# A mixture-of-experts decoder on one core: seven of eight experts sorted by token count, four of them in plain float32, gathers one expert ahead

## The chip, the cores and the metric

The kernel runs on one core of one Trainium2 chip. The time is device microseconds of one execution, and lower is better. The profile is of one execution of its own.

## What is computed

Two decoder layers on 256 tokens of 1024 features: an RWKV-7 time mix with a dense SwiGLU, then an RG-LRU block with a top-2-of-8 expert SwiGLU, and a last norm. All weights and activations are float32. The change lies in the expert layer alone:

```python
def moe_swiglu(h, w_router, b_router, w_gu, w_d):      # h: 256 tokens x 1024
    t = h.reshape(B * T, D)
    logits = t @ w_router + b_router                     # 8 experts
    top_v, top_i = lax.top_k(logits, 2)
    comb = einsum('nk,nke->ne', softmax(top_v), one_hot(top_i, 8))
    for e in range(8):                                   # w_gu[e]: 1024 x 7168, w_d[e]: 3584 x 1024
        out = out + comb[:, e, None] * swiglu(t, w_gu[e], w_d[e])
```

256 tokens with two experts each make 512 rows, 64 for each expert in the mean. With the inputs as drawn by the reference the counts of experts 0 to 7 are 59, 75, 55, 76, 73, 57, 51 and 66.

## The kernel before

The expert layer is the last stage. It runs 8 positions `e` one after the other, each of `NJ` = 7 steps `j` over 512 of the 3584 hidden columns: 56 steps `s` in all. A step takes 6 tiles of 1 MB of weights: two for gate, two for up, two for down (the down tiles of step `s` come behind the gate and up tiles of step `s+1`). `Stream` (line 100) loads them through SP's queue into a ring of 12 buffers; a load is issued when the tile 12 places before it is free.

Positions come in two kinds.

- A *large* position holds up to 128 tokens. Each tile is cut in two pieces of 1024 columns. ScalarE rounds a piece to float32r (`wh`), VectorE makes the rest (`wl`), and TensorE adds three float32r products (`mm3`). The step has 72 products of 512 columns and four transposes of the hidden tile (`hp`). A raw tile is free when VectorE has split its second piece. `Stream.next` emits the splits four pieces ahead, with five pairs of buffers.
- A *small* position (those in `SMALL` = 2, 5, 7) holds up to 64 tokens. Its tiles go to TensorE as they are, as plain float32 products of 512 columns whose two halves of the output columns fill the two halves of the array. A raw tile is free when TensorE has read it. There is nothing to split.

Experts 0 and 1 run at positions 0 and 1. Experts 2 to 7 are ranked by their token counts on VectorE (`t_rank`, `t_sel`), and `TURN` gives the rank of each position 2 to 7, so that the three with the fewest tokens come to positions 2, 5 and 7. The order of kinds is L L S L L S L S. From position 2 on the address of a weight load comes from a register of SP, which `turns()` (emitted behind step 4) loads from `turn_i`. A count over 64 in a small position or over 128 in a large one sets `cmx`, and the kernel then runs `overflow` (line 269) at its end, for each expert that has too many tokens, with all its weights loaded again.

Tokens are gathered by a product with a 0/1 matrix `Pm`. Two neighbouring positions are gathered together: 32 products of 256 columns in float32r (`gather_mm`: 8 feature tiles, high and low part, two token tiles), then ScalarE scales and shifts (`gather_mod`), rounds (`gather_out`), and VectorE makes the low part. For positions 0 and 1 this is `first_gather`, in front of the stage; for the others `gather(pair)` is emitted at the last step of an odd position. `scatter_cols` transposes `Pm` for the way back. At the end of a position, `expert_out` weighs the down result, splits it and adds it onto the tokens (`onto`: `sc` tiles, two products for each of four parts).

Small work (`expert_out`, `choice`, `scatter_cols`, the ranking) stands in the list `chores`; `chore()` takes one from it in front of each piece of a large position, and as often in a small one. Everything that isn't held to program order is ordered by the tile scheduler; each engine then runs its own queue in order. The PSUM tiles of `hp`, `gp` (gather), `sc` and `ptp` take banks 4 and 5 by turns.

Of the kernel before, what the change touches and what calls it, by code (L numbers as in the profile page):

```python
# [16 lines left out]
P = 128  # L17
# [11 lines left out]
SMALL = (2, 5, 7)  # L29
HALF = 64  # L30

TURN = (3, 0, 1, 4, 2, 5)
# [310 lines left out]
def kernel_body(tc, io, out, dbg=None):  # L343
# [18 lines left out]
    with ctx:  # L362
# [1042 lines left out]
        turn_i = rw.tile([P, E - 2], I32, name="turn_i")  # L1405
# [5 lines left out]
        crank, turnf = wrs[:, 2, 0:E - 2], wrs[:, 3, 0:E - 2]  # L1411
        oscr = cst2[:, 0:72].rearrange("p (i a b) -> p i a b", i=2, a=E - 2)
        sel = cst2[:, 72:108].rearrange("p (a b) -> p a b", a=E - 2)
# [247 lines left out]
        def as_numbered(w, e, *j):  # L1661
            return w[(e, *j)]

        add_steps(0, 2 * NJ, as_numbered)
# [15 lines left out]
        def onehot(Pm, i, pair, behind=None):  # L1680

            for z in range(2):
                e = 2 * pair + z
                pm, at, ps_, ms_ = Pm[:, i, z, :], iota, *((posq, mskq) if pair else (posm, msk))
                if e in SMALL:

                    pm, at = pm.rearrange("p (a c) -> p a c", a=2), iota[:, None, 0:HALF].broadcast_to([P, 2, HALF])
                ins = V.tensor_scalar(pm, at, ps_[:, i, e:e + 1], ms_[:, i, e:e + 1], ALU.is_equal, ALU.mult)
                if behind is not None:
                    order(tc, ins, behind)  # L1690
            return ins
# [38 lines left out]
        gps = [pg.tile([P, 2, 2 * CAP], F32, tag="g", name=f"gp0{k2}") for k2 in range(4)]  # L1730
        Pm = rp.tile([P, 2, 2, CAP], F32R, name="Pm0")
# [72 lines left out]
        def first_gather(i, ks, parts=range(2)):  # L1804
            for k in ks:
                for z in parts:
                    gather_mm(gps[k // 2][:, k % 2, :], (hh, hl)[z], i, k, Pm, i == 0 and k % 2 == 0 and z == 0,
                              i == 1 and k % 2 == 1 and z == 1)
# [80 lines left out]
        ma = ml.enter_context(tc.tile_pool(name="moe2", bufs=1))  # L1889

        spare = cst3
        xg, xfs = {}, {}
# [4 lines left out]
        def gather_mod(pair, k2, ps, eng=(0, 1)):  # L1897

            a = ma.tile([P, 2, 2 * CAP], F32R, tag=f"xh{k2}", name=f"xh{pair}{k2}")
            b = ma.tile([P, 2, 2 * CAP], F32R, tag=f"xl{k2}", name=f"xl{pair}{k2}")  # L1900
            xg.setdefault(pair, []).append((a, b))

            if pair == 0:
                xf = rr[:, 2 * k2:2 * k2 + 2, :]
            else:
                xf = (ma.tile([P, 512], F32, tag="xf", name=f"xf{pair}{k2}") if k2 % 2 == 0 else spare).rearrange("p (k c) -> p k c", k=2)
            xfs[k2] = xf
            for kk in range(2):
                k = 2 * k2 + kk
                if eng[kk]:  # L1910
                    V.tensor_scalar(xf[:, kk, :], ps[:, kk, :], mod(1, 4, k), mod(1, 3, k), ALU.mult, ALU.add)
                else:
                    S.activation(xf[:, kk, :], ps[:, kk, :], AF.Identity, bias=mod(1, 3, k), scale=mod(1, 4, k))

        def gather_out(pair, k2):

            a, b = xg[pair][k2]
            zs = [z for z in range(2) if 2 * pair + z not in SMALL]
            cs = slice(zs[0] * CAP, (zs[-1] + 1) * CAP)
            S.copy(a[:, :, cs], xfs[k2][:, :, cs])  # L1920
            V.tensor_tensor(b[:, :, cs], xfs[k2][:, :, cs], a[:, :, cs].bitcast(F32), ALU.subtract)
            for z in range(2):
                if z not in zs:
                    S.copy(xsm[2 * pair + z][:, 2 * k2:2 * k2 + 2, :], xfs[k2][:, :, z * CAP:z * CAP + HALF])

        for k2 in range(4):
            if k2 == 0:
                gather_mod(0, 0, gps[0])
            if k2 < 3:
                gather_mod(0, k2 + 1, gps[k2 + 1])  # L1930
            gather_out(0, k2)
            if k2 == 2:
                more(1)
                later()
# [8 lines left out]
        def scatter_cols(pair, z, eng):  # L1943
            ps = pdn.tile([P, 2, P], F32, tag="m", name=f"ptp{pair}{z}", bufs=2)
            for i in range(2):
                TE.transpose(ps[:, i, :], Pms[pair][:, i, z, :].bitcast(F32), ident)
            PT = ma.tile([P, 2, P], F32R, tag="PT", name=f"PT{pair}{z}", bufs=2)
            eng(PT, ps)
            PTs[2 * pair + z] = PT

        def choice(pair, i):
            if i == 0:
                Pms[pair] = mb.tile([P, 2, 2, CAP], F32R, tag="Pm", name=f"Pm{pair}")
            onehot(Pms[pair], i, pair, st.split[1])


        N6 = E - 2
        o6 = oscr.rearrange("p a b c -> p (a b c)")[:, 0:N6 * N6].rearrange("p (b c) -> p b c", b=N6)

        def t_rank():  # L1960

            a_, b_ = cnt[:, None, 2:E].broadcast_to([P, N6, N6]), cnt[:, 2:E, None].broadcast_to([P, N6, N6])
            V.tensor_tensor(o6, a_, b_, ALU.is_equal)
            V.tensor_tensor(o6, o6, lt8[:, 2:E, 2:E], ALU.mult)
            V.tensor_tensor(sel, a_, b_, ALU.is_gt)
            V.tensor_tensor(o6, o6, sel, ALU.add)
            V.tensor_reduce(crank, o6, AX.X, ALU.add)

        def t_sel():
            for k, r in enumerate(TURN):  # L1970
                V.tensor_scalar(sel[:, k, :], crank, float(r), None, ALU.is_equal)
            V.tensor_tensor(o6, sel, iota[:, None, 2:E].broadcast_to([P, N6, N6]), ALU.mult)
            V.tensor_reduce(turnf, o6, AX.X, ALU.add)
            V.tensor_copy(turn_i, turnf)

        def t_sort(dst, src):
            V.tensor_copy(dst[:, :, 0:2], src[:, :, 0:2])
            V.tensor_tensor(oscr, src[:, :, None, 2:E].broadcast_to([P, 2, N6, N6]),
                            sel[:, None, :, :].broadcast_to([P, 2, N6, N6]), ALU.mult)
            V.tensor_reduce(dst[:, :, 2:E], oscr, AX.X, ALU.add)  # L1980

        def t_cap():

            V.memset(cap, float(CAP))
            V.tensor_scalar(cap[:, 2:E], crank, float(N6 - len(SMALL)), None, ALU.is_ge)
            V.tensor_scalar(cap[:, 2:E], cap[:, 2:E], float(HALF - CAP), float(CAP), ALU.mult, ALU.add)
# [7 lines left out]
        def turns():  # L1994
# [3 lines left out]
            def by_turn(w, e, *j):  # L1998
                if e < 2:
                    return as_numbered(w, e, *j)  # L2000
                return w[(bass.ds(regs[e - 2], 1), *j)].rearrange("o p n -> (o p) n")

            add_steps(2 * NJ, len(steps), by_turn)
# [3 lines left out]
        def gather(pair):  # L2007

            for k2 in range(KT // 2):
                ps = pdn.tile([P, 2, 2 * CAP], F32, tag="m", name=f"gp{pair}{k2}", bufs=2)  # L2010
                for kk in range(2):
                    for z, src in enumerate((hh, hl)):
                        for i in range(2):
                            gather_mm(ps[:, kk, :], src, i, 2 * k2 + kk, Pms[pair], z == 0 and i == 0, z == 1 and i == 1)
                gather_mod(pair, k2, ps, (0, 0))
                gather_out(pair, k2)

        def gu_half(e, ps):
            xs = xg[e // 2]
            for q in range(4):  # L2020
                chore()
                wh, wl = st.next()
                for kk in range(2):
                    k = 2 * q + kk
                    cs = slice((e % 2) * CAP, (e % 2) * CAP + CAP)
                    mm3(ps, xs[q][0][:, kk, cs], xs[q][1][:, kk, cs],
                        wh[:, kk * 512:(kk + 1) * 512], wl[:, kk * 512:(kk + 1) * 512], k == 0, k == KT - 1)

        def gu_small(e, ps):

            for h in range(2):
                w = [st.next() for _ in range(2)]
                for k4 in range(4):
                    chore()
                    k = 4 * h + k4
                    for z in range(2):
                        mm(ps[z * HALF:(z + 1) * HALF], xsm[e][:, k, :], w[z][:, k4 * 512:(k4 + 1) * 512], k == 0, k == KT - 1)
# [44 lines left out]
        def expert_out(e):  # L2082
# [5 lines left out]
            def weigh(n):  # L2088
                yg[n] = ma.tile([P, 512], F32, tag="xf", name=f"yg{e}{n}") if n == 0 else spare
# [9 lines left out]
            def onto(n, i):  # L2099
# [7 lines left out]
                V.scalar_tensor_tensor(xt[:, i, sl], ps, (cmbq if e > 1 else cmb)[:, i, e:e + 1], xt[:, i, sl], ALU.mult, ALU.add)  # L2107
# [14 lines left out]
        def expert_out_small(e):  # L2122

            yg = ma.tile([P, 512], F32, tag="xf", name=f"yg{e}")
# [74 lines left out]
        for s, (e, j) in enumerate(steps):  # L2199
# [5 lines left out]
            if s == 0:  # L2205
                for z in range(2):
                    scatter_cols(0, z, S.copy)
# [197 lines left out]
```

## Time and profile before

| | us |
|---|---|
| median of 3 runs | 1537.98 (1536.16 to 1539.76) |
| the profiled execution | 1536.94 |
| its span, first to last instruction | 1534.8 |
| of it, up to the first gate product of the expert layer | 617.15 |
| expert layer up to its last down product | 902.6 |
| rest of the span | 15.0 |

The rows that the prediction uses stand in numbered groups in a later section. In rows of groups of instructions, the columns are the line (96 is the helper that records each operation), engine, operation, output <- inputs by the program's names, shapes, count, then busy us and mean ns of one, then idle us of the engine before them and what ended it. Products of one accumulation are pipelined, so the mean of one is longer than the distance from one to the next; that is read from the chain of waits, where a line gives start, duration and count of a run of products.

### The profile page before, as it was taken

To read this page: it belongs to the slowest core of one execution; us is meant where nothing else is said; L and a number is where in the kernel's file an instruction comes from. 1 tells how busy PE (TensorE), PEld (TensorE's weight loads), DVE (VectorE), ACT (ScalarE), POOL (GpSimd) and SP (SyncE) were. 2 spreads that over 40 slices of the span, in tenths; PEclk is the share of its full clock that TensorE was granted. 3 is DMA by queue.
4 is the path that set the end of the run, shared out by engine and by line. 5 is a ranking of instruction groups with operands and counts; after the bars stand their busy time and mean duration, and the time that the engine had idled before them with its cause. 6 is when DMAs were issued, how large, how long until landed. Compare 5 with 4: busy or idle time off the path is not lost.

```text
span 1534.8 us, 21180 instructions
## 1 busy us (share of the span) xinstructions
PE 1455.3 (95%) x7887; PEld 1070.1 (70%) x7887; DVE 1102.6 (72%) x1612; ACT 834.5 (54%) x1202; POOL 52.7 (3%) x44
## 2 busy tenths in 40 slices
PE   4998898999999898999999999999999999999996
PEld 3774684999999897878888534688788533688432
DVE  7788977788886887999999412887898512788302
ACT  3657434444444675877777412676777303577101
POOL 3011700000000000000000000000000000000000
PEclk9999989999999999999999999999999999999999
DMA  9563336988988345799999799999899899999796
GB/s 377 182 233 137 111 111 269 364 301 325 339 303 321 138 158 198 268 364 370 366 354 359 316 416 421 421 421 386 313 363 375 332 391 421 420 421 386 302 420 256
DMA packets 69936, 488.55 MB, mean 318 GB/s; under 512 B 8000, under 2 KB 8384, under 8 KB 11968
## 3 DMA queue, kind: packets, MB, share of 16 engines
q1 hardware_dynamic: 69824, 487.11, 82.2%
q8 instruction: 64, 1.05, 0.3%
q14 instruction: 48, 0.39, 0.1%
HBM read 486.03 MB, written 1.05 MB: 317 GB/s over the span
## 4 chain that ended last, share of the span: by engine, by line
PE 81%; DVE 8%; DMA 5%; ACT 4%; issue 1%; SPq 0%; POOL 0%; DVEq 0%; ACTq 0%
PE mg L96 20%; PE dn L96 16%; PE mu L96 13%; PE fgu L96 11%; PE fd L96 5%; DMA rw<-moe_gu 4%; PE psr L96 2%; PE linx L96 2%; DVE rq L96 2%; PE u L96 1%; PE hp L96 1%; DVE wl L96 1%; PE psk L96 1%; PE sc L96 1%; DMA rq<-ada 1%
## 5 line engine op out<-in xcount | busy, mean ns | idle before, releaser
L96 DVE TENSOR_TENSOR wl<-rw,wh 128x1024 fp32r<-128x1024 f32 x528 | 626.6, 1221 | 81.9 <-ACT wh L96 75.5
L96 ACT CAST wh<-rw 128x1024 fp32r<-128x1024 f32 x528 | 542.5, 1051 | 188.6 <-PE fgu L96 44.6
L96 PE MATMUL mg<-rw,condr 128*64 128x512 f32 x672 | 160.6, 595 | 2.2 <-DMA rw<-moe_gu 2.2
L96 DVE TENSOR_TENSOR sl<-sl,mg 64x512 f32<-64x512 f32 x21 | 14.5, 692 | 163.4 <-ACT sl L96 163.4
L96 PE MATMUL fgu<-fxh,wh 128*128 128x256 f32 x448 | 127.2, 285 | 1.2 <-ACT fxh L96 1.2
L96 PE MATMUL fgu<-fxl,wh 128*128 128x256 f32 x448 | 127.2, 284 | 0.0
L96 PE MATMUL fgu<-fxh,wl 128*128 128x256 f32 x448 | 126.6, 283 | 0.0
L96 PE MATMUL mg<-wl,xh 128*128 128x512 f32 x280 | 113.8, 406 | 7.9 <-DVE wl L96 7.8
L96 PEld LDWEIGHTS mg<-rw,condr 128*64 128x64 f32 x672 | 49.5, 137 | 98.2 <-issue 92.0
L96 PE MATMUL mg<-wh,xh 128*128 128x512 f32 x280 | 111.0, 396 | 2.9 <-ACT wh L96 2.9
L96 PE MATMUL dn<-wl,hTh 128*128 128x512 f32 x280 | 111.3, 398 | 0.6 <-DVE wl L96 0.6
L96 PE MATMUL dn<-wh,hTl 128*128 128x512 f32 x280 | 111.6, 399 | 0.0
L96 PE MATMUL mu<-wh,xh 128*128 128x512 f32 x280 | 111.3, 397 | 0.0
L96 PE MATMUL mg<-wh,xl 128*128 128x512 f32 x280 | 110.5, 394 | 0.2 <-DVE xl L96 0.2
L96 PE MATMUL mu<-wl,xh 128*128 128x512 f32 x280 | 110.2, 394 | 0.0
L96 PE MATMUL mu<-wh,xl 128*128 128x512 f32 x280 | 109.7, 392 | 0.0
L96 PE MATMUL dn<-wh,hTh 128*128 128x512 f32 x280 | 99.8, 398 | 0.7 <-ACT hTh L96 0.7
L96 ACT ACTIVATE sl<-mg 128x512 f32<-128x512 f32 (+1 forms) x56 | 32.9, 588 | 123.8 <-PE mg L96 123.7
L96 PEld LDWEIGHTS fgu<-fxh,wh 128*128 128x128 f32 x448 | 84.8, 190 | 2.0 <-ACT fxh L96 1.6
L96 PE MATMUL dn<-rw,hTh 128*64 128x512 f32 x336 | 84.9, 599 | 0.5 <-ACT hTh L96 0.5
L96 PEld LDWEIGHTS fgu<-fxl,wh 128*128 128x128 f32 x448 | 84.9, 190 | 0.7 <-issue 0.5
L96 PEld LDWEIGHTS fgu<-fxh,wl 128*128 128x128 f32 x448 | 85.2, 190 | 0.2 <-issue 0.2
(416 smaller groups left out, 2464.9 us busy)
## 6 DMA issues: line engine op xcount, KB each, us to landing
rw<-moe_gu SPq DMA_DIRECT2D x224, 1024.0 KB, 7.5
rw<-moe_d SPq DMA_DIRECT2D x106, 1024.0 KB, 7.9
rw<-ffn_gu SPq DMA_DIRECT2D x28, 1024.0 KB, 7.4
rw<-ada SPq DMA_DIRECT2D x28, 1024.0 KB, 7.8
rq<-ada SPq DMA_DIRECT2D x19, 1024.0 KB, 5.1
rw<-ffn_d SPq DMA_DIRECT2D x14, 1024.0 KB, 6.3
rw<-lru_in SPq DMA_DIRECT2D x8, 1024.0 KB, 7.4
rw<-moe_d SPq DMA_DIRECT2D x12, 512.0 KB, 15.0
```

Of the source, the lines that this page charges most:

```text
L96: r = f(*a, **k)
```

## The change

- Position 0 holds expert 7 (`FIRST`). The experts 0 to 6 are ranked, and positions 1, 3, 5 and 7 hold the four with the fewest tokens as small ones: L S L S L S L S. The ranking works on 7 x 7 instead of 6 x 6. `turns()` stands behind step 3 instead of 4.
- Tokens are gathered for one position at a time: 32 products of 128 columns for a large position, of 64 for a small one. `first_gather` serves position 0 alone. The gather for position `e+1` goes through `chores` while position `e` runs: from its step 2 in a large one, from step 1 in a small one, in two blocks of 16 products, with ScalarE's part as further chores. A large position's gather goes into two PSUM tiles of four feature tiles each, a small one's into one.
- `scatter_cols` is called for each position.
- The tiles of gathered tokens are half as wide, and small positions share one. The room goes to one more ring buffer (`rawD`): 13.

```diff
-SMALL = (2, 5, 7)
+FIRST = E - 1
+SMALL = (1, 3, 5, 7)
-TURN = (3, 0, 1, 4, 2, 5)
+TURN = (3, 0, 4, 1, 5, 2, 6)
...
-        add_steps(0, 2 * NJ, as_numbered)
+        add_steps(0, NJ, of_first)
...
         def gather_mm(o, src, i, k, Pm, start, stop):
-            mm(o, src[:, i, k * P:(k + 1) * P], Pm[:, i, :, :].rearrange("p z c -> p (z c)"), start, stop)
+            mm(o, src[:, i, k * P:(k + 1) * P], Pm[:, i, 0:o.shape[-1]], start, stop)
...
-        gps = [pg.tile([P, 2, 2 * CAP], F32, tag="g", name=f"gp0{k2}") for k2 in range(4)]
-        Pm = rp.tile([P, 2, 2, CAP], F32R, name="Pm0")
+        gps = [pg.tile([P, 4, CAP], F32, tag="g", name=f"gp0{k4}") for k4 in range(2)]
+        Pm = rp.tile([P, 2, CAP], F32R, name="Pm0")
...
-        first_gather(1, range(2), range(1))
-        first_gather(1, range(2), range(1, 2))
-        first_gather(1, range(2, 8))
+        first_gather(1, range(4), range(1))
+        first_gather(1, range(4), range(1, 2))
+        first_gather(1, range(4, 8))
...
+        st.grow(ml.enter_context(tc.tile_pool(name="rawD", bufs=1)))
-        spare = cst3
+        spare, other = cst3, condr[:, KT * HALF:D]
-        xsm = {e: condr[:, n * 512:(n + 1) * 512].rearrange("p (k c) -> p k c", k=KT) for n, e in zip((0, 1, 0), SMALL)}
+        xsm = condr[:, 0:KT * HALF].rearrange("p (k c) -> p k c", k=KT)
...
-        def gather(pair):
-            for k2 in range(KT // 2):
-                ps = pdn.tile([P, 2, 2 * CAP], F32, tag="m", name=f"gp{pair}{k2}", bufs=2)
-                for kk in range(2):
-                    for z, src in enumerate((hh, hl)):
-                        for i in range(2):
-                            gather_mm(ps[:, kk, :], src, i, 2 * k2 + kk, Pms[pair], z == 0 and i == 0, z == 1 and i == 1)
-                gather_mod(pair, k2, ps, (0, 0))
-                gather_out(pair, k2)
+        def gather(e, k0, n):
+            c = HALF if e in SMALL else CAP
+            if k0 % (512 // c) == 0:
+                gp[e] = pdn.tile([P, 512 // c, c], F32, tag="m", name=f"gp{e}{k0}", bufs=2)
+            for k in range(k0, k0 + n):
+                for z, src in enumerate((hh, hl)):
+                    for i in range(2):
+                        gather_mm(gp[e][:, k % (512 // c), :], src, i, k, Pms[e], z == 0 and i == 0, z == 1 and i == 1)
+        def gathered(e, k0):
+            if e in SMALL:
+                for k in (k0, k0 + 1):
+                    gather_mod(k, xsm[:, k, :], gp[e][:, k, :], 0)
+                return
+            if k0 % 4 == 0:
+                xf_[0] = (spare if k0 else other).rearrange("p (k c) -> p k c", k=4)
+            for k in (k0, k0 + 1):
+                gather_mod(k, xf_[0][:, k % 4, :], gp[e][:, k % 4, :], 0)
+            gather_out(e, k0 // 2, xf_[0][:, k0 % 4:k0 % 4 + 2, :])
+        def fetch(e):
+            c = [lambda i=i: choice(e, i) for i in range(2)]
+            if e in SMALL:
+                c += [lambda k=k: gather(e, k, 4) for k in (0, 4)]
+                c += [lambda k=k: gathered(e, k) for k in range(0, KT, 2)]
+            else:
+                for h in (0, 4):
+                    c += [lambda h=h: gather(e, h, 4)] + [lambda k=k: gathered(e, k) for k in (h, h + 2)]
+            return c
...
-            if s == 4:
+            if s == 3:
                 turns()
-            if e % 2 == 1 and j == NJ - 3 and e < E - 1:
-                chores.extend([lambda i=i: choice((e + 1) // 2, i) for i in range(2)])
-            if e % 2 == 1 and j == NJ - 1 and e < E - 1:
-                gather((e + 1) // 2)
-            if e % 2 == 0 and e > 0 and j == 2:
-                chores.extend([lambda z=z: scatter_cols(e // 2, z, V.tensor_copy) for z in range(2)])
+            if j == (1 if e in SMALL else 2):
+                if e > 0:
+                    chores.append(lambda e=e: scatter_cols(e, V.tensor_copy if e in SMALL else S.copy))
+                if e < E - 1:
+                    chores.extend(fetch(e + 1))
```

## Rows read from the trace of the kernel before

**Rows 1.** The page: busy time of TensorE, clock and DMA rate in 40 slices.

```profile
PE 1455.3 (95%) x7887; PEld 1070.1 (70%) x7887; DVE 1102.6 (72%) x1612; ACT 834.5 (54%) x1202; POOL 52.7 (3%) x44
...
GB/s 377 182 233 137 111 111 269 364 301 325 339 303 321 138 158 198 268 364 370 366 354 359 316 416 421 421 421 386 313 363 375 332 391 421 420 421 386 302 420 256
```

**Rows 2.** Stretches, first gate product to the next position's: length, engines, clock, DMA.

```profile
core 0: us, PE busy (x) PEld busy (x) DVE busy (x) ACT busy (x) POOL busy (x), PEclk, DMA share, GB/s
617.15:733.15 116.00, 115.84 (x515) 93.42 (x513) 109.30 (x130) 93.41 (x103) 0.00 (x0) 1.00 0.93 345
733.15:858.49 125.34, 125.34 (x574) 102.37 (x572) 114.23 (x113) 99.88 (x115) 0.00 (x0) 1.00 0.96 352
858.49:946.75 88.26, 85.11 (x389) 31.32 (x389) 15.13 (x22) 10.78 (x21) 0.00 (x0) 1.00 0.95 393
946.75:1076.77 130.02, 126.95 (x560) 99.37 (x561) 106.85 (x107) 91.20 (x107) 0.00 (x0) 0.99 0.99 405
1076.77:1201.44 124.67, 122.91 (x546) 98.74 (x544) 110.80 (x110) 91.39 (x103) 0.00 (x0) 1.00 0.95 354
1201.44:1299.34 97.90, 92.96 (x417) 35.35 (x417) 18.41 (x29) 19.93 (x39) 0.00 (x0) 1.00 0.94 383
1299.34:1424.21 124.87, 121.79 (x532) 94.58 (x532) 105.30 (x102) 85.86 (x93) 0.00 (x0) 1.00 1.00 408
1424.21:1519.77 95.56, 91.76 (x401) 33.48 (x400) 15.65 (x20) 13.92 (x23) 0.00 (x0) 0.98 0.90 364
1519.77:1534.80 15.03, 3.82 (x8) 1.18 (x8) 7.34 (x14) 4.14 (x11) 0.00 (x0) 0.78 0.21 75
```

**Rows 3.** Stretches of single steps, and of the first two steps of small positions.

```profile
786.26:803.31 17.05, 17.05 (x77) 13.91 (x76) 15.72 (x15) 13.50 (x14) 0.00 (x0) 1.00 1.00 370
1246.05:1256.88 10.83, 10.83 (x54) 3.68 (x52) 0.69 (x1) 0.96 (x2) 0.00 (x0) 1.00 1.01 422
858.49:888.94 30.45, 29.62 (x130) 12.48 (x129) 11.22 (x15) 4.98 (x9) 0.00 (x0) 1.00 0.85 346
1201.44:1235.20 33.76, 31.45 (x125) 12.89 (x126) 13.22 (x19) 7.27 (x10) 0.00 (x0) 1.00 0.80 309
1424.21:1458.82 34.61, 32.66 (x126) 13.96 (x126) 12.20 (x15) 7.26 (x10) 0.00 (x0) 0.95 0.77 297
```

**Rows 4.** Timeline of TensorE where positions meet: waits in brackets.

```profile
1211.51 0.40 PE L96 MATMUL hp<-vec,sl 64*128 64x64 f32 x3 [1.41 <-DVE sl L96]
1299.34 0.50 PE L96 MATMUL mg<-wh,xh 128*128 128x512 f32 x1 [1.42 <-ACT wh L96]
```

**Rows 5.** Stretches of the last three steps of position 5, which carry a gather.

```profile
1256.88:1269.56 12.68, 12.15 (x62) 4.54 (x59) 0.69 (x1) 1.33 (x3) 0.00 (x0) 1.00 1.01 422
1269.56:1284.54 14.98, 14.40 (x69) 5.78 (x68) 1.54 (x3) 4.21 (x10) 0.00 (x0) 1.00 1.01 419
1284.54:1299.34 14.80, 13.28 (x61) 4.78 (x61) 1.56 (x4) 5.20 (x12) 0.00 (x0) 1.00 1.02 423
```

**Rows 6.** Chain of waits: start, us, runs of products (`gp`, then `psr` in plain float32).

```profile
848.96 1.88 PE gp L96 x16
...
62.91 3.65 PE psr L96 x16
```

**Rows 7.** Timeline of TensorE in front of the stage: eight products of 8 columns.

```profile
607.62 1.06 PE L96 MATMUL lgp<-wrs,rr 128*128 128x8 f32 x8 [0.68 <-ACT rr L96]
```

**Rows 8.** Groups of instructions from 640 us on: what follows a gather.

```profile
L96 ACT ACTIVATE xf<-gp,mods 128x256 f32<-128x256 f32 x12 | 6.3, 563 | 7.1 <-PE gp L96 7.1
L96 ACT CAST xh<-xf 128x256 fp32r<-128x256 f32 x6 | 2.4, 403 | 1.0 <-PE mu L96 0.9
```

**Rows 9.** Stretches of the first gather, and its products one by one.

```profile
611.00:614.00 3.00, 2.41 (x11) 2.07 (x10) 3.00 (x8) 1.49 (x3) 0.00 (x0) 0.50 0.85 300
614.00:617.00 3.00, 3.00 (x16) 3.00 (x15) 2.28 (x16) 1.74 (x4) 0.00 (x0) 0.51 0.03 14
...
614.73 0.41 PE L96 MATMUL gp<-Pm,mhh 128*128 128x256 f32 x1
614.95 0.41 PE L96 MATMUL gp<-Pm,mhl 128*128 128x256 f32 x1
```

**Rows 10.** SP's load of the order of experts, and what made it.

```profile
L96 DVE CAST turn_i<-wrs x1: 165/165/165, 641.6 to 641.6; 128x6 int32<-128x6 f32 x1
L1996 SPq TENSOR_LOAD <-turn_i x1: 928/928/928, 663.2 to 663.2; - x1
```

More of the change, by code (lines that the diff above doesn't have):

```diff
@@ L1678, in lo_mm, with onehot @@
                     w[0][:, kk * 512:(kk + 1) * 512], w[1][:, kk * 512:(kk + 1) * 512], k == 0, k == KT - 1)
[L1680 to L1691, printed above, removed]
+        def onehot(Pm, i, e, behind=None):
+            pm, at, ps_, ms_, c = Pm[:, i, :], iota, *((posq, mskq, e) if e else (posm, msk, FIRST))
+            if e in SMALL:
+                pm, at = pm.rearrange("p (a c) -> p a c", a=2), iota[:, None, 0:HALF].broadcast_to([P, 2, HALF])
+            ins = V.tensor_scalar(pm, at, ps_[:, i, c:c + 1], ms_[:, i, c:c + 1], ALU.is_equal, ALU.mult)
+            if behind is not None:
+                order(tc, ins, behind)
         def gather_mm(o, src, i, k, Pm, start, stop):
-            mm(o, src[:, i, k * P:(k + 1) * P], Pm[:, i, :, :].rearrange("p z c -> p (z c)"), start, stop)
+            mm(o, src[:, i, k * P:(k + 1) * P], Pm[:, i, 0:o.shape[-1]], start, stop)
         def finish(i, n, pool, tag):
@@ L1915, in gather_out @@
[L1915 to L1932, printed above, removed]
+        xsm = condr[:, 0:KT * HALF].rearrange("p (k c) -> p k c", k=KT)
+        def gather_mod(k, dst, ps, eng):
+            if eng:
+                V.tensor_scalar(dst, ps, mod(1, 4, k), mod(1, 3, k), ALU.mult, ALU.add)
+            else:
+                S.activation(dst, ps, AF.Identity, bias=mod(1, 3, k), scale=mod(1, 4, k))
@@ new lines, in gather_out @@
+        def gather_out(e, k2, xf):
+            a = ma.tile([P, 2, CAP], F32R, tag=f"xh{k2}", name=f"xh{e}{k2}")
+            b = ma.tile([P, 2, CAP], F32R, tag=f"xl{k2}", name=f"xl{e}{k2}")
+            xg.setdefault(e, []).append((a, b))
+            S.copy(a, xf)
+            V.tensor_tensor(b, xf, a.bitcast(F32), ALU.subtract)
+        for k2 in range(5):
+            if k2 < 4:
+                for k in (2 * k2, 2 * k2 + 1):
+                    gather_mod(k, rr[:, k, 0:CAP], gps[k // 4][:, k % 4, :], k % 2)
+            if k2 > 0:
+                gather_out(0, k2 - 1, rr[:, 2 * k2 - 2:2 * k2, 0:CAP])
+            if k2 == 3:
@@ L2088, in weigh @@
             def weigh(n):
-                yg[n] = ma.tile([P, 512], F32, tag="xf", name=f"yg{e}{n}") if n == 0 else spare
+                yg[n] = spare if n else other
                 V.tensor_tensor(yg[n], dps[e][n], gt2[:, n * 512:(n + 1) * 512], ALU.mult)
@@ L2205, in kernel_body @@
             if s == 0:
-                for z in range(2):
-                    scatter_cols(0, z, S.copy)
+                scatter_cols(0, S.copy)
                 weights()
```

103 lines of the change are left out of this document (45 added, 58 removed).

## Prediction, made blind

> **What bounds the kernel now.** I read the page first. TensorE is busy for 95% of the span, and from about 600 us on the loads run at 302 to 421 GB/s [rows 1]. 421 is the highest rate of any slice, so I take it for saturation. Both could be the bound, so I cut the expert layer at the first gate product of each position and asked for each stretch [rows 2]. The reader is to see three things. Large positions take 116.0 to 130.0 us, with TensorE busy for nearly all of it. Small ones take 88.3 to 97.9 us. The loads reach 408 GB/s in the large position that follows a small one (1299 to 1424), but 345 to 354 in a large one that follows a large one, where the ring fills and SP waits for room.
>
> Then single steps [rows 3]. A large step is 17.05 us, TensorE busy throughout, VectorE 15.72 and ScalarE 13.50. A small step is 10.83 us of pure TensorE work. Each step needs 6 MB, 6.29 million bytes, or 14.9 us at 421 GB/s. So large steps are bound by TensorE and small ones outrun the loads: seven large and seven small steps are 195 us of TensorE against 209 us of loads.
>
> Read as far as this, the change looks worth a great deal: the 42 small steps that alternate with large ones would be bound by loads alone. The rows of where positions meet say otherwise. The first two steps behind a large position take 33.76 and 34.61 us instead of twice 10.83 [rows 3], for the down products of the large step, the way back of its tokens, and waits on VectorE such as 1.41 us [rows 4]. With that a small position takes 33.8 + 5 x 10.83 = 88 us of TensorE, and a large one behind it 124.9 us [rows 2]. The pair is 213 us without any gather, over the 209 us of its loads. So I count along TensorE, and take the loads as hidden unless the sum falls under 209 us a pair.
>
> **The change part by part.** I sum from the first gate product (617.15) to the last down product (1519.77), and leave the 15.03 us behind it as they are [rows 2].
>
> *One large position less, one small more.* The new order has one large position at the front, three large ones behind small ones, and four small ones behind large ones. Gone are two large positions that follow large ones; new are one large behind a small and one small behind a large. Base values, without a gather:
> - Front: 116.0 us [rows 2].
> - Large behind small: 124.9 us as from 1299 to 1424. The one from 947 to 1077 is 130.0, but it carries a pair's gather. From 124.9 I take 0.4 us for half of the `Pm` transposes, which go to the small position: 124.5.
> - Small behind large: 33.8 us for the first two steps (I leave the 34.61 aside, since the granted clock fell to 0.95 there; the third, 30.45, stands behind a gather that gave VectorE time to catch up [rows 3]); four steps of 10.83; a last of 10.83 and the 1.42 us that the next large position waits for its first `wh` [rows 4]; 0.4 us for the transposes. Sum 33.8 + 43.3 + 12.3 + 0.4 = 89.8.
> - Last: 95.6 us as it is [rows 2], with 0.4 for transposes, less 1.8 because the loads, late there, have one more buffer. One tile at 421 GB/s is 2.5 us; I take somewhat less. 94.2.
>
> *The gathers.* Before, a pair's gather has 32 products of 256 columns, 16 of them in 1.88 us, so 0.12 us each [rows 6]. After, every position has its own 32 products, with half or a quarter of the columns. No row shows a float32r product of fewer than 256 columns, so I bound it. From below: `lgp` has 8 columns, and still eight take 1.06 us, 0.13 each, with a new stationary tile for each [rows 7]. So narrow products don't fall under about 0.12. From above: plain float32 products of 256 columns come every 0.228 us, two to a product [rows 6], so 128 columns would cost 0.228 and 64 columns 0.114. For 64 columns both ends meet: 32 x 0.12 = 3.8 us, and 0.3 for the interruption, 4.1. For 128 columns the ends are 3.8 and 7.3 us. I take the upper, because the float32r rows at one column per cycle are all 256 columns wide or wider, and the narrow rows are plain float32, at two cycles per column for each pass. A gather in a small position also breaks the pairs of half-array products: the three steps that carry one take 42.46 us [rows 5] where 3 x 10.83 + 1.42 = 33.9 were due, so it costs 8.5 us, 3.8 for the products and some 1.2 for each of its four blocks. Taking 0.9 for each of two longer blocks, since part of that is counted in the products, a large position's gather costs 7.3 + 1.8 = 9.1 us, or 5.6 at the lower end.
>
> The Trainium skill (TensorE: Matmul & The Clock Gate, "Back-to-back issue gap") gives about 81 ns for a product of 128 columns with its weight load, and 131 ns at 512 columns. Here 512-column pairs fill a 17.05 us step of 72 [rows 3], over 0.23 each, so the page's figures don't hold for float32 operands; by it a large gather would be 2.6 us (an estimate), and the sum 14 us lower. Its section "LDWEIGHTS" puts a load of 128 columns at 107 ns, whatever the product behind it; that speaks against narrow gathers, and the `lgp` row agrees.
>
> *The first gather* runs at a granted clock of 0.50 to 0.51, at 1.2 GHz: 16 products 0.21 us apart [rows 9]. At twice the cost 16 of them add 3.4 us; part of it lies beside ScalarE's and VectorE's work on the first tiles. Between 0 and 5, I take 2.
>
> *Moved chores.* ScalarE's part of a small position's gather is eight activations. For 256 columns one takes 0.563 us [rows 8], so eight are at most 4.5 us in a large position whose steps leave ScalarE 17.05 - 13.50 = 3.5 us each: behind them on ScalarE wait the next `wh`, with pieces split ahead. I count nothing, and at most 1 us for each of four positions if that cover is gone. In a small position ScalarE and VectorE are all but idle (0.96 and 0.69 us a step). `turns()` a step earlier: SP's load took 0.93 us at 663.2, of numbers made at 641.6 [rows 10]. One step earlier is 646, still behind them; queued behind it are loads for steps that are 30 us away. Nothing. The ring's 13th buffer is worth 2.5 us once where loads are late, and that is in the last position only.
>
> *Sum.* 617.15 + 2.0 (first gather) + 120.1 (front, 116.0 + 4.1) + 3 x 98.9 (small, 89.8 + 9.1) + 3 x 128.6 (large, 124.5 + 4.1) + 94.2 = 1516.0, against 1519.8: 3.8 us less. The same account of the kernel before closes at 1519.8, for it is read from its stretches. So the large position saved pays 124.9 - 89.8 and some stalls, and 23 us of it go to gathers. The span becomes 1531.0. The profiled execution (1536.94) lies 2.1 us over its span, and the median 1.0 over that: 1534.2.
>
> **The rivals.**
>
> *Narrow gathers are cheap*, 0.12 us a product. For it: the rows of 256 columns cost just that, and a weight load is hidden. Against: no narrow float32r row. Then the first gather costs nothing and the three large gathers 3.5 us less each: 3.8 + 2.0 + 10.5 = 16.3 us less, 1521.7.
>
> *The bank wait.* A large position's gather takes two PSUM tiles, and its second block of 16 products, in TensorE's queue ahead of the small position's own products, can't start until a bank is free, nor can the next `hp`. What empties a bank is four activations on ScalarE and two roundings, at most 4 x 0.563 + 2 x 0.403 = 3.1 us [rows 8], with everything else of TensorE queued behind. If both halves of each wait for all of it rather than the 0.9 us that I count, it is 2.2 x 6 = 13 us more: 1547. It decides from about 1.7 us a half on, where the gain of 3.8 is gone and 1 more lost. Against it: the blocks are some steps of the chore list apart, and the waits before a block of the old gather are about half a microsecond (0.53 us of idle from 1256.88 to 1269.56 [rows 5]).
>
> *The meetings get better.* If VectorE isn't late where a small position begins, as from 858 to 889 (30.45 us [rows 3]), four of them give 13 us: 1521. Against it: that one stood behind a gather at the end of the large position, and the new gathers stand at its third step.
>
> *It isn't what it says.* Were there more than 64 tokens in one of the four small positions, `overflow` would run: seven steps of 24 plain float32 products of 512 columns, 4 x 0.228 us each, 153 us more, 1688. The counts of experts 0 to 6 are 59, 75, 55, 76, 73, 57, 51, so the four are 59, 57, 55 and 51, and the first has 66 of 128. Very unlikely.
>
> **How the numbers follow.** The forecast 0.42, cheap gathers 0.27, the bank wait 0.16, better meetings 0.10, overflow 0.02, others 0.03. The range takes in both rivals that are faster, with some 4 us for the unknown waits, and the bank wait: 1517 to 1548. A measurement here tells about 0.2%, 3 us, from no change. The forecast lies just beyond that: of its 0.42 I give 0.22 to faster, 0.13 to the same, 0.07 to slower. With 0.25 and 0.10 from the faster rivals it is faster 0.57, same 0.20, slower 0.23 (the bank wait, overflow and the rest among it).
>
> **What would show it.** In the profile of the changed kernel: seven blocks of 32 gather products, 0.23 us apart at 128 columns and 0.12 at 64; small positions of about 99 us and large ones behind them of about 129; loads under 400 GB/s in most slices, with SP waiting for room and TensorE hardly ever for a landing; first two steps of a small position near 34 us. The forecast is wrong if TensorE waits for landings in small positions, if ScalarE ends the waits in front of `gp` or `hp` with over 1.7 us a half, or if narrow products come every 0.12 us.

## The result, and the profile after

The changed kernel takes 1530.49 us (median of five, 1529.51 to 1530.81) against 1537.98 (five, 1536.02 to 1539.76): a ratio of 0.995, 95% interval 0.9935 to 0.9964. That is 7.5 us faster, where 3.8 were forecast. The profiled execution took 1529.51 us, and its span is 1527.7.

On the page of the changed kernel the busy time of TensorE and the rates answer to [rows 1]; the line below them is the chain that ended last, by engine.

```profile
PE 1449.1 (95%) x7847; PEld 1024.9 (67%) x7847; DVE 1001.2 (66%) x1519; ACT 752.4 (49%) x1139; POOL 52.9 (3%) x44
...
GB/s 370 191 234 138 111 104 266 373 291 327 337 304 322 135 163 213 265 304 369 357 390 421 421 421 369 298 387 421 421 420 370 292 393 421 421 421 362 297 418 250
...
PE 85%; DVE 9%; ACT 3%; DMA 2%; issue 1%; SPq 0%; POOL 0%; ACTq 0%; DVEq 0%
```

TensorE is as busy as before, and the chain is still its own. The dips to 292 to 298 GB/s are the first steps of small positions, which take TensorE longest for their tiles: in position 3 three steps of 53.8 us. In the rows below, `mg` and `mu` are the gate and up products, `dn` the down products, `sl` the activated hidden tile, `hp` its transposes, and `hTh` what ScalarE copies of them for the down products.

The positions of the changed kernel in the columns of [rows 2], position 0 to 4 and 7 (5 and 6 take 98.80 and 129.76 us; behind the last down product come 15.53):

```profile
618.18:740.38 122.20, 122.20 (x543) 99.03 (x543) 108.93 (x119) 95.33 (x110) 0.00 (x0) 0.97 0.89 328
740.38:832.62 92.24, 90.25 (x419) 37.28 (x419) 14.97 (x25) 14.03 (x31) 0.00 (x0) 1.00 0.97 389
832.62:960.77 128.15, 125.07 (x562) 97.98 (x563) 106.13 (x102) 88.54 (x102) 0.00 (x0) 1.00 1.00 403
960.77:1059.59 98.82, 94.79 (x420) 36.56 (x419) 18.22 (x28) 17.83 (x35) 0.00 (x0) 0.98 0.90 363
1059.59:1189.40 129.81, 126.73 (x563) 99.13 (x563) 106.23 (x102) 88.69 (x102) 0.00 (x0) 0.99 0.99 404
...
1417.96:1512.17 94.21, 91.12 (x403) 33.53 (x402) 15.98 (x21) 13.93 (x23) 0.00 (x0) 0.98 0.89 360
```

Against the forecast (120.1; small 98.9; large 128.6; last 94.2; start 619.15): the start is 1.0 early, position 0 is 2.1 long, position 1 is 6.7 short, position 2 is 0.45 short, positions 3 and 5 fit within 0.1, positions 4 and 6 are 1.2 long each, position 7 fits. The sum is -3.8, and the last down product comes at 1512.17 instead of 1516.0. So the question is not only why the sum was 3.8 off. Position 1 and position 3 do the same work, and they differ by 6.6 us. Their first three steps, up to the end of the gather, differ by more (45.58 against 53.82); steps 3 and 4 of position 1 take 11.38 and 11.91 us, where position 3 has 10.8, and give 1.6 of it back. Three things account for the 8.2, and the chain of waits and the timelines show them.

**The order at the meeting.** The chain of the changed kernel at the start of position 1, then of position 3 (start, us, what):

```profile
740.45 7.02 PE mg L97 x32
747.46 0.59 PE hp L97 x4
748.05 1.00 PE mg L97 x2
749.05 5.76 PE dn L97 x24
...
960.84 1.00 PE mg L97 x2
961.84 0.59 PE hp L97 x4
962.43 7.02 PE mg L97 x30
...
969.48 0.60 ACT sl L97
970.09 1.05 ACT wh L97
971.17 1.24 DVE wl L97
972.45 6.47 PE dn L97 x20
```

and TensorE's timeline there:

```profile
970.85 0.40 PE L97 MATMUL hp<-vec,sl 64*128 64x64 f32 x3 [1.41 <-DVE sl L97]
...
972.45 0.50 PE L97 MATMUL dn<-wl,hTh 128*128 128x512 f32 x1 [0.32 <-DVE wl L97]
```

In position 1 the 24 down products of the large step before follow right behind the first gates, and cover the way from `mg` through `sl` to `hp`. In position 3 TensorE's queue has nearly all gates and then the `hp` of the small step's own hidden tile first. It stands still for 1.41 us until VectorE has made `sl`, then for 0.32 more until `wl` is made, and only then come the down products, but for two. The 1.41 us is the wait of [rows 4]. Positions 5 and 7 have it too.

TensorE's queue is only one side of it. The timelines of ScalarE, in front of position 1 and in position 3, and of VectorE in position 3:

```profile
739.09 1.06 ACT L97 CAST wh<-rw 128x1024 fp32r<-128x1024 f32 x1 [0.34 <-PE dn L97]
...
969.48 0.59 ACT L97 ACTIVATE sl<-mg 64x512 f32<-64x512 f32 x1 [6.42 <-PE mg L97]
970.09 3.90 ACT L97 CAST wh<-rw 128x1024 fp32r<-128x1024 f32 x4
...
970.10 0.69 DVE L97 TENSOR_TENSOR sl<-sl,mg 64x512 f32<-64x512 f32 x1 [6.32 <-ACT sl L97]
```

The 24 down products need four pieces of weights. In position 1 the last of the four is rounded before the position begins. In position 3 all four stand in ScalarE's queue behind the small step's `sl`, which waits 6.42 us for the gates. So these down products weren't ready to run there: the first `wl` is made at 972.41. VectorE wasn't behind with its work either; it had been idle for 6.32 us.

**The gather in pieces.** The chain of the changed kernel: the gather in position 1 (128 columns), the one in position 2 (64 columns), and the beginning of the one in position 3 (128 columns):

```profile
776.28 1.93 PE gp L97 x16
...
782.33 1.93 PE gp L97 x16
...
892.89 3.38 PE gp L97 x31
...
992.61 0.48 PE gp L97 x3
993.09 1.87 PE dn L97 x8
994.96 0.81 PE gp L97 x6
```

A product of 64 columns takes 0.11 us and one of 128 columns 0.12. That is the price of 256 columns before [rows 6]. But in positions 3 and 5 the 32 products lie in eight pieces between half-array products.

**The clock.** Stretches of the changed kernel: behind the gather in position 0, in position 3 behind the waits above, at the start of position 2 and at that of position 4:

```profile
670.00:672.00 2.00, 2.00 (x6) 1.53 (x5) 0.00 (x0) 0.90 (x4) 0.00 (x0) 0.50 0.95 356
974.00:976.00 2.00, 2.00 (x6) 1.61 (x5) 1.80 (x2) 0.00 (x0) 0.00 (x0) 0.50 1.01 426
835.00:837.00 2.00, 2.00 (x11) 1.61 (x10) 2.00 (x2) 2.00 (x3) 0.00 (x0) 1.00 0.99 414
1062.00:1064.00 2.00, 2.00 (x6) 1.54 (x5) 2.00 (x2) 2.00 (x3) 0.00 (x0) 0.50 1.03 430
```

At 0.50 (1.2 GHz) a 512-column product comes every 0.43 us instead of 0.23. Positions 2 and 4 begin with the same waits (1.47 us for `wh`, 0.76 for `wl`). In position 2 the clock stays at 1.00, in position 4 it falls, and the position is 1.66 us longer (129.81 against 128.15). From 624 us on the changed kernel has six such stretches, at 670, 974, 1062, 1202, 1290 and 1430. The kernel before has two, at 948 and 1436. Each costs some 1.7 us.

### The profile page after: what moved, and what is told of

The parts are those of the page before. It is cut to its first block, busy times and chain, and to the rows that moved or that the text cites. A ratio compares the mean times of both kernels' runs of the same rounds, so it can differ in the third digit from the quotient of the medians.

```text
span 1527.7 us, 20895 instructions
## 1 busy us (share of the span) xinstructions
PE 1449.1 (95%) x7847; PEld 1024.9 (67%) x7847; DVE 1001.2 (66%) x1519; ACT 752.4 (49%) x1139; POOL 52.9 (3%) x44
## 4 chain that ended last, share of the span: by engine, by line
PE 85%; DVE 9%; ACT 3%; DMA 2%; issue 1%; SPq 0%; POOL 0%; ACTq 0%; DVEq 0%
PE mg L97 24%; PE dn L97 17%; PE fgu L97 11%; PE mu L97 10%; PE fd L97 5%; PE gp L97 2%; PE psr L97 2%; PE linx L97 2%; DVE rq L97 2%; DVE s L97 2%; PE hp L97 1%; PE u L97 1%; PE sc L97 1%; DVE wl L97 1%; DMA rq<-ada 1%; PE psk L97 1%
## 5 line engine op out<-in xcount | busy, mean ns | idle before, releaser
L97 DVE TENSOR_TENSOR wl<-rw,wh 128x1024 fp32r<-128x1024 f32 x444 | 529.0, 1220 | 93.1 <-ACT wh L97 87.4
L97 ACT CAST wh<-rw 128x1024 fp32r<-128x1024 f32 x444 | 456.4, 1051 | 164.9 <-PE fgu L97 45.0
L97 PE MATMUL mg<-rw,condr 128*64 128x512 f32 x896 | 217.7, 595 | 0.0
L97 PE MATMUL dn<-rw,hTh 128*64 128x512 f32 x448 | 108.4, 599 | 1.0 <-ACT hTh L97 1.0
L97 PE MATMUL mg<-wl,xh 128*128 128x512 f32 x224 | 92.4, 413 | 9.2 <-DVE wl L97 9.2
L97 PE MATMUL mg<-wh,xh 128*128 128x512 f32 x224 | 90.7, 405 | 4.9 <-ACT wh L97 4.4
L97 PE MATMUL dn<-wh,hTl 128*128 128x512 f32 x224 | 91.0, 406 | 0.0
L97 PE MATMUL mu<-wh,xh 128*128 128x512 f32 x224 | 89.1, 398 | 0.0
L97 PE MATMUL mu<-wl,xh 128*128 128x512 f32 x224 | 88.0, 393 | 0.0
L97 PE MATMUL mu<-wh,xl 128*128 128x512 f32 x224 | 87.7, 391 | 0.0
```

Source lines behind the costliest of these rows:

```text
L97: r = f(*a, **k)
```

## The experiments

Every time is a median, beside runs of the kernel before on the same chip; ratios are against that kernel. Its median was 1537.07 to 1538.9 us beside the experiments, so between two of them times tell nothing under some 2 us; there the stretches of the positions decide. To be compared: the changed kernel, 1530.49 us.

### The thirteenth buffer

```diff
-        st.grow(ml.enter_context(tc.tile_pool(name="rawD", bufs=1)))
```

> The changed kernel (1530.5 us) with 12 ring buffers instead of 13. If TensorE sets the pace and loads matter in the last small position alone, one tile (2.5 us at 421 GB/s) is lost there at most once: 1530 to 1533. Rival: the loads end the small positions. Then each of the four is 2.5 us longer, and the time is about 1540.

1532.03 us, ratio 0.9965 (0.995 to 0.9979). Positions 0 to 6 stay within 0.3 us; only the last grows, from 94.21 to 96.70:

```profile
1417.27:1513.97 96.70, 92.28 (x403) 33.68 (x402) 15.99 (x21) 13.93 (x23) 0.00 (x0) 0.98 0.89 362
```

So up to there the loads don't set the time, and the buffer is worth 2.5 us in the last position, where 1.8 were counted.

### Half of the large gathers

```diff
-                for z, src in enumerate((hh, hl)):
+                for z, src in enumerate((hh, hl)[:1 if e not in SMALL else 2]):
```

(with the `stop` flag to match)

> The changed kernel, whose large positions 2, 4 and 6 gather only the high part of their tokens: 16 products instead of 32 (the low part is left out of what is computed). If the cost of a gather is its products at 0.12 us, three positions save 16 x 0.12 = 1.9 us each, 5.8 in all: about 1524.7. If it is products at the forecast 0.228 us: 11 us, 1519.5. Rival: it is the pieces into which the gather is cut, each of which breaks a pair of half-array products, so that the 9 us of a gather fall by half: 14 us, about 1516.5.

1523.06 us, ratio 0.9907 (0.9891 to 0.9923), between what the prices of 0.12 and of 0.228 had led to expect. Positions 3 and 5 go from 98.8 to 95.29: 3.5 us for 16 products, 0.22 each. Read alone, this is the forecast's price of 0.228. But the chain has the products at 0.12 where they stand together, so nearly half of the 0.22 is what the pieces cost besides. In position 1, where the gather is whole, the same 16 products bring 1.53 us (92.24 to 90.71), 0.10 each. That gain doesn't show in the sum, because the clock now falls at the start of position 2, as it does in position 4: 129.71 instead of 128.15.

```profile
830.91:960.62 129.71, 126.62 (x562) 99.17 (x562) 106.24 (x102) 88.71 (x102) 0.00 (x0) 0.99 0.99 397
960.62:1055.91 95.29, 91.27 (x403) 34.61 (x402) 18.21 (x28) 17.84 (x35) 0.00 (x0) 0.98 0.91 369
```

### 128 columns everywhere

```diff
-            c = HALF if e in SMALL else CAP
+            c = CAP
```

(the small positions then gather 128 columns in two PSUM tiles, and use 64)

> The changed kernel (1530.5 us), whose small positions gather with 128 columns a product instead of 64, in two PSUM tiles as a large position does. If a narrow product costs what its stationary tile costs to load (0.11 to 0.12 us in the changed kernel at 64 and at 128 columns), four gathers of 32 products add about 1.4 us: 1530 to 1533. If it costs two cycles a column for each of two passes, as the forecast took it: 32 x 0.114 x 4 = 14.6 us more, 1545.

1532.37 us, ratio 0.9958 (0.994 to 0.9976): 1.9 us more for 128 products of twice the width. At the forecast's prices (0.228 instead of 0.12) it would be 13.8. The chain in position 2 has 30 of these wide products in a row:

```profile
895.42 3.30 PE gp L97 x30
```

That is 0.110 us each, as for 64 columns (3.38 for 31). So between 64 and 128 columns the width doesn't set the price. The Trainium skill (TensorE: Matmul & The Clock Gate, "LDWEIGHTS") reckons the load of a stationary tile by its own columns, which makes 107 ns for 128 (an estimate from its formula). The distance of 0.110 us fits that; no run shows that the load is what sets it.

This run also parts the waits from the clock:

```profile
964.03:1061.31 97.28, 93.24 (x419) 35.44 (x418) 18.22 (x28) 17.84 (x35) 0.00 (x0) 1.00 0.93 372
```

Position 3 has the waits of 1.41 and 0.32 us as before, but the clock stays at 1.00, and it is 1.54 us shorter than in the changed kernel; so are positions 5 and 7. The clock falls twice in each of positions 2, 4 and 6 instead (131.3 to 131.4 us). That makes six falls, as many as in the changed kernel, in other places. The wait alone doesn't decide whether the clock falls.

### The gather at the end of a position

```diff
-                if e < E - 1:
-                    chores.extend(fetch(e + 1))
+            if j == NJ - 3 and e < E - 1:
+                chores.extend(fetch(e + 1)[:2])
+            if j == NJ - 1 and e < E - 1:
+                for f in fetch(e + 1)[2:]:
+                    f()
```

> The changed kernel with each gather in one go behind the last gate and up products of the position before, where the kernel before had it, instead of in chores from step 1 or 2 on. If pieces between small products are the cost, a large position's gather falls from 9 to 32 x 0.12 + 1.5 = 5.3 us, and three of them save 11: about 1519. Rival: what follows the gather on ScalarE and VectorE (about 3 us for each half of it) then stands in front of the next position, and seven of these take back 1 to 3 us each: 1526 to 1540.

1535.24 us, ratio 0.998 (0.997 to 0.9989), 4.8 us slower than the changed kernel. Position 1 grows by 4.3 us. Position 2 grows by 3.4, at a clock of 0.97: it falls there at 838 and again at 858. It also tests the forecast's reading that a gather in front of a meeting lets VectorE catch up. Here one stands in front of position 3 (7 of its products right before the last down products, at 962.22), and the wait is there all the same:

```profile
978.80 0.40 PE L97 MATMUL hp<-vec,sl 64*128 64x64 f32 x3 [1.40 <-DVE sl L97]
```

The reading falls. Late in a position the gather is cut into pieces as well (5, 10 and 1 at the end of position 1), so its place alone doesn't keep it whole, and what a whole one there would bring (1519 us were expected) isn't shown.

### The large step's down products first

The first step of each small position keeps program order on TensorE. The edit says no more, but the scheduler orders ScalarE's work with it, as the rows show:

```diff
+            if s > 0:
+                TE.on = e in SMALL and j == 0
```

(and `TE.on = False` behind the loop)

> The changed kernel with TensorE held to program order in step 0 of each small position, so that the down products of the large step run before the transposes of the small step's own hidden tile, as they do in position 1, where the first five steps take 68.9 us instead of 75.5. If the order of issue makes the stall of positions 3, 5 and 7, each gains 3 to 6.6 us: 1511 to 1521. Rival: VectorE is late with the last pieces there, and TensorE waits for them whatever the order: 1529 to 1532.

1518.76 us, ratio 0.9874 (0.9855 to 0.9892): 11.7 us less than the changed kernel. The chain at the start of position 3, ScalarE's timeline there, and the position:

```profile
962.93 7.02 PE mg L97 x32
...
971.21 6.09 PE dn L97 x24
...
958.80 1.05 ACT L97 CAST wh<-rw 128x1024 fp32r<-128x1024 f32 x1 [0.28 <-PE dn L97]
...
971.79 2.00 ACT L97 CAST wh<-rw 128x1024 fp32r<-128x1024 f32 x2
...
962.85:1057.01 94.16, 91.09 (x419) 35.03 (x418) 16.11 (x26) 15.98 (x33) 0.00 (x0) 1.00 0.94 382
```

Positions 3, 5 and 7 lose 4.66, 4.65 and 3.35 us, and position 1, which had this order already, stays (92.60). The 1.41 us wait is gone, and the clock doesn't fall there: position 3 now has 1.00. Two of the four pieces are now rounded in front of the position, the other two behind an `sl` that has nothing to wait for. So the order at the meeting makes the stall, and not a VectorE that is late whatever the order; but whether it is TensorE's order or ScalarE's this run doesn't show, since both changed. Of the 4.66 us TensorE's idle time is 0.96 (2.56 us of it in the first three steps before, with the waits of 1.73; 1.60 now, 0.68 for `hTh` and 0.92 on the way back), the stretch at half clock some 1.7, and the rest, some 2.0, is busy time: the gather lies in six pieces instead of eight. In this execution (1523.07 us, the slowest of four) position 6 takes 134.30 us, because the clock fell there at 1282, 1302 and 1347.

### The same with twelve buffers

The edits of the first and the fifth experiment together.

> down_first (1518.8 us) with 12 ring buffers. In the changed kernel the 13th buffer was worth 1.5 us. If TensorE still sets the pace, the same here: about 1520. Rival: with the small positions 4.6 us shorter the loads end them, each loses up to one tile, 2.5 us, in four places: 1526 to 1529.

1518.16 us, ratio 0.9869 (0.9852 to 0.9885), against 1518.76 with thirteen. Positions 3 and 5 are as long as with thirteen (94.16 and 94.15). The last isn't:

```profile
1407.15:1501.08 93.93, 89.38 (x403) 32.14 (x402) 13.89 (x19) 12.06 (x21) 0.00 (x0) 1.00 0.92 372
```

It is 3.1 us longer than with thirteen (90.86), and its gate products wait twice for a landing, 1.8 us in all. The medians hide that: positions 4 and 6 were 1.6 and 4.6 us shorter in the profiled execution, at a clock of 1.00 and 0.99 instead of 0.99 and 0.95. So shorter small positions don't make the loads the bound, but for the last one, as with twelve buffers in the changed kernel.

### Small positions in program order

```diff
+            if s > 0:
+                TE.on = e in SMALL
```

> As down_first (1518.8 us), but TensorE is held to program order in all seven steps of each small position, so that a large position's gather runs in two unbroken blocks of 16 products. If pieces between half-array products are what a gather costs beyond its products, positions 3 and 5 fall from 94.2 to about 90.7 us, and position 1 a little: 1510 to 1514. Rival: the mixed order hides waits (for the hidden tile on ScalarE, for the parts of the way back) that stand bare in program order, half a microsecond in each of 28 small steps: 1525 to 1535.

1513.70 us, ratio 0.9839 (0.9822 to 0.9855). All of a small position is now in order, the gather too. The chain in position 3, and the position:

```profile
997.36 1.95 PE gp L97 x16
...
1003.09 1.93 PE gp L97 x16
...
962.27:1054.56 92.29, 87.67 (x420) 33.81 (x419) 16.32 (x26) 16.03 (x33) 0.00 (x0) 1.00 0.98 404
```

The eight pieces have become two blocks, but position 3 takes 92.29 us where 90.7 were expected. Strict order costs in the later steps: TensorE waits 25 times for `hTh`, 13.2 us in all, where the changed kernel does so twice (1.0 us).

### The first three steps in order

So I kept program order where it pays, from the meeting to the end of the gather, and left the other four steps to the scheduler:

```diff
+            if s > 0:
+                TE.on = e in SMALL and j < 3
```

> As small_in_order (1513.7 us), but TensorE is held to program order only in the first three steps of each small position, those with the large step's down products, the way back and the gather. In small_in_order the four later steps are 11.43 us each, with 0.5 us of wait for the hidden tile on ScalarE, where the scheduler's order takes 10.84. If that is all, 0.5 x 4 x 4 = 8 us come back: about 1506. Rival: with shorter small positions the loads end them, and large positions start later: 1510 to 1514.

1507.06 us (1505.65 to 1507.29), ratio 0.9794 (0.9771 to 0.9818): 30 us faster than the kernel before, and 23.4 faster than the changed one. Positions 3, 4 and 7:

```profile
961.05:1051.89 90.84, 88.23 (x420) 34.05 (x419) 16.32 (x26) 16.06 (x33) 0.00 (x0) 1.00 0.98 405
1051.89:1180.03 128.14, 125.06 (x563) 97.99 (x563) 108.44 (x104) 90.58 (x104) 0.00 (x0) 1.00 1.00 403
...
1400.53:1489.13 88.60, 86.88 (x403) 31.31 (x402) 14.07 (x19) 12.06 (x21) 0.00 (x0) 1.00 0.93 381
```

Position 3 goes from 98.82 through 94.16 (down products first) to 90.84 (gather whole as well). So the order of the first step brings 4.66 us, with a fall of the clock in it, and that of the next two 3.32. Of the 3.32 TensorE's idle time is 0.46, since the way back no longer waits; the rest is busy time, with the gather in two blocks instead of six pieces. Position 4 is back at 128.1, at a clock of 1.00. Behind 624 us the clock falls twice, at 669 and 1291, where the changed kernel has six falls: that is some 7 of the 23.4 us. The waits for `hTh` are down to 9, 5.2 us in all.

### The kernel before, with the same order

The same three lines in the kernel before, whose small positions are 2, 5 and 7.

> The kernel before (1538 us) with the same order in the first three steps of its three small positions. Its positions 5 and 7 have the stall, position 2 hasn't. If the stall is one of order alone, two positions gain 3 to 4.7 us: 1529 to 1532, and the changed kernel in the same order, with one more such position and one large position less, is ahead of it by more than the 7.5 us measured. Rival: the loads bind here, and nothing changes: 1536 to 1539.

1527.65 us, ratio 0.9932 (0.9909 to 0.9955). Its small positions 2, 5 and 7 go from 88.26, 97.90 and 95.56 [rows 2] to:

```profile
860.19:946.25 86.06, 83.77 (x389) 31.91 (x388) 15.22 (x22) 10.81 (x21) 0.00 (x0) 1.00 0.96 396
...
1199.55:1293.21 93.66, 89.83 (x417) 34.32 (x416) 16.41 (x27) 18.08 (x37) 0.00 (x0) 1.00 0.98 407
...
1419.62:1509.04 89.42, 87.42 (x401) 31.48 (x400) 13.66 (x18) 12.06 (x21) 0.00 (x0) 1.00 0.96 391
```

1527.65 us is below the 1529 to 1532 expected: position 2, whose meeting was good already, gains 2.2 us as well.

With that order in both, the change is worth 1527.65 - 1507.06 = 20.6 us instead of 7.5. What it lost as it stands went to the meetings (the kernel before has two bad ones, the changed kernel three), to gathers cut in pieces, and to the clock: it falls six times against two as they stand, and twice against once in this order, which is some 5 of the 13 us.

## Why the prediction was right, and where it was wrong

**What bounds it: right.** TensorE sets the pace, and loads are hidden. On the page no gate product waits for a landing any more (2.2 us in the kernel before), and with twelve buffers only the last position changes. The last position's 94.2 came out at 94.21, with the buffer's part 2.5 us instead of 1.8.

**The price of a narrow product: wrong.** The forecast took the upper end, 0.228 us for 128 columns, "because the float32r rows at one column per cycle are all 256 columns wide or wider". It is 0.11 to 0.12, the lower end, the rival's price; `lgp` [rows 7] had been the nearer row, a product with a new stationary tile each time. Products every 0.12 us are one of the three signs that the forecast itself named for being wrong. For the three large gathers that is 3 x 3.5 = 10.5 us too much.

**The interruptions: undersized.** The forecast counted 1.8 us for a large gather, two blocks at 0.9. In positions 3 and 5 there are eight pieces. The first three steps take 53.82 us there; less 33.76 and 10.83 [rows 3], 0.4 for the transposes and 1.7 for the clock, that leaves 7.1 for the gather, 3.2 beyond its products at 3.9. (Half the products took 3.5 off.) In position 1 the gather is whole and the meeting good: 45.58 less 30.45, 10.83 and 0.4 leaves 3.9, its products alone. Its first three steps are thus 8.5 us short of the forecast, 5.2 by the gather and 3.3 by the meeting, but the other four take 46.66 where 44.7 were counted. The 6.7 us are what is left of both.

The half-array products show what a piece costs. Two products that fill the two halves start together and take one slot of 0.43 us. Where other work cuts in, two are left that run one after the other: two alone take 1.00 us (in the trace they start at 985.74 and 986.22), and 14 take 3.58, about as long as eight slots instead of seven.

**The clock: not counted.** The forecast took the clock as 1.00 behind the first gather. Six stretches at 0.50, some 1.7 us each, are 10 us, where the kernel before has two. One of the six is in the row of the last position, which the forecast took over (0.98); the other five, 8.5 us, it didn't count. In positions 4 and 6 they are the 1.2 us by which the forecast fell short; in 3 and 5 they happen to fill what the gather came out below it. Positions 3 and 5 thus fit to 0.1 us by two errors of opposite sign, and the sum of -3.8 is worth less as evidence for its terms than it looks. Some 17 us were forecast that didn't come (10.5 for products, 1.8 and 3.3 for the blocks and the meeting of position 1, 1.0 at the start), and some 15 came that weren't forecast (2.8 for pieces in positions 3 and 5, 8.5 for five falls of the clock, 1.6 for it at the start of position 0, 1.9 in the later steps of position 1). That the time came out so near is luck in part.

**The first gather and position 0.** The start came 1.0 us later than before, not 2.0, so half as much of the slow products lay on the path. But the clock stayed at 0.50 until some 621 us (before, until 617), some 1.6 us in position 0, and fell again behind the 31 gather products at 665, 1.7 more. Position 0 is 2.1 us longer than forecast, not 3.3: the gather's products took 3.5 us of the 4.1 counted, and the last 0.6 stays open.

**The stall at the meetings: its price right, its cause wrong.** The forecast gave each small position behind a large one 33.8 us for two steps. Position 7, which carries no gather, takes 35.7, and 33.6 without the clock's 1.7 and 0.4 for the transposes. But the forecast blamed VectorE's lateness; it explained the good meeting at 858 [rows 3] by a gather that stood in front. The chain of the kernel before, read there again, shows another cause, the order of the first steps:

```profile
858.56 7.02 PE mg L96 x32
865.58 0.60 PE hp L96 x4
...
866.84 1.20 PE dn L96 x4
```

That is position 1's order in the changed kernel, and the one at 1201 in the kernel before (2 gates, 4 `hp`, 30 gates, then the wait of [rows 4]) is position 3's. ScalarE's order goes with it there too: the four pieces are rounded from 855.83 to 859.72 in front of the good meeting, and from 1210.76 on, behind `sl`, in the bad one. The rows were in the trace; the forecast compared lengths where it should have compared the order of the work. The rival "the meetings get better" was half right: one meeting of four did. Down products first shows that the order makes the stall, by taking it away.

**The chores and the bank wait.** ScalarE's part of the gathers cost nothing that shows: at a clock of 1.00 a large position is 128.15, against 128.6. The view of waits lists none on ScalarE in front of `gp` or `hp`, so the bank wait did not come. The order of experts arrived in time, and `overflow` did not run.

**Open.** Why the scheduler puts the down products first in position 1 and not in positions 3, 5 and 7 was not tried, nor which of the two orders, TensorE's or ScalarE's, makes the stall. Why the same waits bring the clock down at position 4 and not at position 2 isn't known either.

## What to carry to other kernels

Where two phases meet, compare the order of the work on the bound engine and on those that feed it, not just the length of the stretch. Here the large step's last four pieces stood behind the small step's own `sl`, and its down products behind the small step's `hp`. That cost up to 4.7 us a time, with a fall of the clock in it, while ScalarE and VectorE stood idle for 6.4 and 6.3 us. These float32r products, each with a new stationary tile, took 0.11 us at 64 and at 128 columns; so halve the number of such products, not their width. And hold program order only where the order matters (three steps of seven: 1507.06 us; all seven: 1513.70; none: 1530.49).

## What the hardware showed

- A float32r product with a new stationary tile of 128 columns takes 0.11 us at 64 and at 128 moving columns and 0.12 at 256.
- Cutting into a run of half-array products is dear where it breaks pairs. 32 of them take 6.87 us, 0.43 a pair, but two that start one after the other take 1.00, and 14 take 3.58, eight times 0.43 and a little. The Trainium skill (TensorEngine Tiling (Array Packing), "Key Properties") says that a change of the tiling mode drains TensorE; the rows fit that, with some 0.15 us for it (32 products take 6.87 us where half-array products follow, and 7.02 where full-array ones do).
- The granted clock fell to 0.50 behind waits of 1.4 us (at 974, 1062, 1202, 1290 and 1430, not at 833), and once behind 31 narrow products in a row with TensorE busy all the time (the stretch at 670). With 128 columns everywhere it stayed at 1.00 behind the same waits in positions 3, 5 and 7. Where it fell, a wait of 1.7 us cost as much again.
